# High and low parts of the tokens side by side: one matmul of 512 columns with the weights' high part in place of two of 256

## The chip, the cores and the metric

One core of one Trainium2 chip. The metric is the device time of one execution in microseconds; times are medians of repeated runs.

## What is computed

A decoder trunk of two layers on 256 tokens of width 1024, all in float32. Layer 0 mixes tokens by latent attention, layer 1 by block attention with a learned bias by distance; with 256 tokens there is one block, so it is causal attention over all keys. Behind each mixer stands an MLP with a squared ReLU:

```python
for i in range(DEPTH):
    h = rms_norm(x, attn_norm[i])
    x = x + mixer(h, ...)            # ends in out @ w_o, 1024 x 1024
    h = rms_norm(x, mlp_norm[i])
    a = relu(h @ w_in)               # 1024 x 4096
    x = x + (a * a) @ w_out          # 4096 x 1024
```

## The kernel before, in words

**Three products for one.** Weights and activations are split into a high part in float32r and the rest, also float32r. A product of two split numbers is `mm3` (L87): high by high, low weight by high token, high weight by low token, three matmuls that add into the same 256 columns of PSUM. The weight block of 128x128 is the loaded operand, the 256 tokens stream past it. In the projections (`lat_mm`, `proj0`, `proj1`) it is the other way round: tokens are loaded, 320, 384 or 512 weight columns stream (`lat_end(latq[t], ...)` streams 384).

**Weights.** All weights come in units of 128x1024 through one list, in order of use. For each, SP issues a DMA into `raw` (four buffers), ACT casts it to `wh` (`hi`, L150) and DVE subtracts to get `wl` (`lo`, L159); wh and wl have seven buffers each. `fill(n)` calls `lo` and `hi` n times. The program is recorded by hand in one order; each engine executes its instructions in that order. So where `fill` stands among the other operations decides what DVE and ACT do first.

**The MLP** (`mlp`, L874 on) runs in two halves r of 16 blocks of 128 hidden features. Each half has a w_in stage of eight steps j, counted from 0 (`first`, L882): two blocks of features, 2 x 8 x 3 matmuls into the two halves of one PSUM bank. Then ACT takes the relu out of PSUM (L900), DVE multiplies it with PSUM (the square-up, L902), ACT casts to a's high part (L904), DVE subtracts to get the low part (L905). In layer 0 and 1 alike, steps 1 to 4 of the first half also square x on ACT (L277), and POOL adds the squares up (L279); behind step 6 a matmul with ones sums over partitions and DVE makes the scale (L919, L920). The w_out stage has eight blocks d of 16 x 3 matmuls (`a` by w_out); DVE multiplies the sum with the scale (y, L936), and POOL adds it to x (L938) in the first half. In the second half `finish` adds it to x and makes h for the next stage, or writes the output.

**Layer 0's MLP also makes layer 1's bias.** In step 5 DVE makes small tables (`bias_tables`, L951 on). Then, once per w_out block, DVE compares positions to a step table `st` (L974); one block later eight small bf16 matmuls of 96 columns read that table, and DVE adds their sums to `bias` in six operations (L987). Blocks 0 to 7 of the first w_out stage make a table each; four more follow in the second half.

**The output projections** (`run_heads`): `o` gathers four blocks of 128 features head by head, `col` makes the other four; each ends in `out_residual`, which adds PSUM to x (L592), makes h's high part on ACT (L586) and its low part hTl on DVE (L588). The first w_in step of the MLP goes through k from 0 to 7 for both feature blocks at once and so wants the last h late.

Of the kernel before, what the change touches and what calls it, by code (L numbers as in the profile page):

```python
# [26 lines left out]
H = 8  # L27
# [33 lines left out]
def trunk(ctx: ExitStack, tc: tile.TileContext, A, out):  # L61
# [189 lines left out]
    hTh = const.tile([P, KD, S], F32R)  # L251
    hTl = const.tile([P, KD, S], F32R)
    room(const, "hT")

# [267 lines left out]
    def head_tiles(l):  # L522

        cm = ExitStack()
        pool = cm.enter_context(tc.tile_pool(name=f"heads{l}", bufs=1))
        r = []
        for c in range(2):
            r.append({n: pool.tile([P, *sh], F32, name=f"{n}{c}")
                      for n, sh in (("k", (HG, S)), ("q", (HG, S)), ("v", (NT, HG, P)))})
        room(pool, f"aT{l}")  # L530
        aT = [pool.tile([P, H, S], F32R, name=f"aT{i}") for i in range(2)]
        return cm, r, aT

    class Head:


        def __init__(self, hd, aT, h, bias, extra=None):
            self.aT = (aT[0][:, h], aT[1][:, h])
# [38 lines left out]
        def values(self):  # L577
            o = ps()
            v, pT = self.hd["v"], self.pT
            mm(o[:, :S], v[:, 0, self.i], pT[:, :S], True, False)  # L580
            mm(o[:, P:S], v[:, 1, self.i], pT[:, S:], False, True)
            nc.scalar.copy(self.aT[0], o[:, :S])
            nc.vector.tensor_sub(self.aT[1], o[:, :S], f32(self.aT[0]))
# [7 lines left out]
    def out_residual(a, d, gname):  # L591
        nc.vector.tensor_add(x[:, d], a, x[:, d])  # L592
        make_h_filled(d, gname)

    def run_heads(hs, proj, post, rows, turn, mid, base, gname, n1):
# [7 lines left out]
        def o(h, ds=range(4)):  # L603
            u = unit(base + h // 2)
            for d in ds:
                if h == 0:
                    accs.append(ps()[:, :S])
                c = (h % 2) * 512 + d * P
                mm3(accs[d], part(u, slice(c, c + P)), hs[h].aT, h == 0, h == H - 1)
                if h == H - 1:  # L610
                    out_residual(accs[d], d, gname)
            if h % 2:
                done(base + h // 2)
# [3 lines left out]
        def col(d, hh):  # L617
            if d not in late:
                late[d] = ps()[:, :S]
            u = unit(base + d)  # L620
            for h in hh:
                mm3(late[d], part(u, slice(h * P, (h + 1) * P)), hs[h].aT, h == 0, h == H - 1)
            if hh[-1] == H - 1:
                done(base + d)
                out_residual(late[d], d, gname)
# [248 lines left out]
    def mlp(l, base, fillers, finish):  # L874

        with tc.tile_pool(name=f"mlp{l}", bufs=1) as pool:
            scale = pool.tile([P, S], F32, name="scale")
            room(pool, "a")
            a = [pool.tile([P, 2 * NPAIR, S], F32R, name=f"a{i}") for i in range(2)]
            sums = SumSquares()  # L880

            def first(b, r, j, split_k):  # L882
                u = [unit(b + 2 * j + i) for i in range(2)]
                if split_k:
                    o = [ps()[:, :S] for _ in range(2)]
                else:
                    p = ps()
                    o = [p[:, f * S:(f + 1) * S] for f in range(2)]
                for f, k in [(f, k) for k in range(KD) for f in range(2)] if split_k else \
                        [(f, k) for f in range(2) for k in range(KD)]:  # L890
# [6 lines left out]
                for f, n in ((0, 1), (1, 1)) if split_k else ((0, 2),):  # L897
                    src = o[f] if split_k else p
                    rl = t2(n * S)
                    nc.scalar.activation(rl, src, AF.Relu)  # L900
                    sq = t2(n * S)
                    nc.vector.scalar_tensor_tensor(sq, src, 0.0, rl, op0=OP.max, op1=OP.mult)  # L902
                    ah, al = (i[:, 2 * j + f:2 * j + f + n].rearrange("p a b -> p (a b)") for i in a)
                    nc.scalar.copy(ah, sq)  # L904
                    nc.vector.tensor_sub(al, sq, f32(ah))  # L905
                done(b + 2 * j + 1)

            for r in range(NR):
                b = base + r * (2 * NPAIR + 2 * KD)
                for j in range(NPAIR):  # L910
# [5 lines left out]
                    if r == 0 and j == 6:  # L916
                        pb = ps()
                        mm(pb[:, :S], ones, s, True, True)
                        nc.vector.tensor_scalar(scale, pb[:, :S], 1.0 / D, EPS, op0=OP.mult, op1=OP.add)  # L919
                        nc.vector.reciprocal(scale, scale)  # L920
                b += 2 * NPAIR
                for d in range(KD):
                    o = ps()[:, :S]
                    for f in range(2 * NPAIR):
                        u = unit(b + 2 * d + f // 8)
                        c = (f % 8) * P
                        mm3(o, part(u, slice(c, c + P)), (a[0][:, f], a[1][:, f]), f == 0, f == 2 * NPAIR - 1)
# [8 lines left out]
                    nc.vector.tensor_tensor(y, o, scale, op=OP.mult)  # L936
# [219 lines left out]
```

## Time and profile before

| | us |
|---|---|
| median of 3 runs | 575.67 (575.59 to 576.53) |
| the profiled execution | 575.54 |
| its span, first to last instruction | 573.4 |
| PE busy, 4346 matmuls | 566.9 |
| PEld (weight loads) busy | 540.6 |
| DVE busy | 406.8 |
| ACT busy | 308.4 |
| POOL busy | 109.5 |

The granted clock of TensorE is 0.999 of its full 2.4 GHz over the span. PE's busy time is that of pipelined matmuls, whose ends are modelled: a matmul of 256 columns is shown as 280 ns long, while the next starts much earlier. What a matmul costs is therefore read as the distance from start to start. Two instructions of DVE or ACT behind each other overlap by some 0.08 us, so there too starts tell more than durations.

### The profile page before, as it was taken

The page shows a single profiled execution, that of the slowest core. Times are in us where ns is not written, and L with a number is a line of the kernel's source. Part 1 is how long each engine was busy: PE and PEld are TensorE (multiplying, and loading weights), DVE is VectorE, ACT ScalarE, POOL GpSimd, SP SyncE. Part 2 cuts the span into 40 slices and gives each one's busy share as a digit, 9 for nine tenths or more (in the row PEclk, how much of TensorE's full clock was granted, in tenths as well). Part 3 has the DMA queues.
Part 4 walks back from the last instruction along what each step waited for, and adds up shares of the span by engine and source line. Part 5 has one row for each costly group of instructions (what it writes and reads, how often), then busy time and mean ns, then how long its engine had stood idle before and what let it go on. Part 6 is the DMA issues. An engine that isn't in the chain of part 4 may idle for free.

```text
span 573.4 us, 10762 instructions
## 1 busy us (share of the span) xinstructions
PE 566.9 (99%) x4346; PEld 540.6 (94%) x4346; DVE 406.8 (71%) x654; ACT 308.4 (54%) x495; POOL 109.5 (19%) x107
## 2 busy tenths in 40 slices
PE   8999999999999999999999999999999999999997
PEld 6888999999999999999988888999999999999996
DVE  5997777588999978687647466776777655666651
ACT  5989676664423455454645466745664434555420
POOL 3882100040223100123413101000221322000100
PEclk9999999999999999999999999999999999999999
DMA  8833455554665555665635544345465575465730
GB/s 289 298 118 124 135 155 156 169 173 154 214 177 177 152 187 179 221 229 174 200 132 177 189 149 146 112 147 184 151 201 197 188 196 173 153 212 174 230 123 29
DMA packets 29265, 99.54 MB, mean 174 GB/s; under 512 B 3904, under 2 KB 4800, under 8 KB 29216
## 3 DMA queue, kind: packets, MB, share of 16 engines
q1 hardware_dynamic: 28736, 97.92, 53.4%
q0 software_dynamic: 336, 0.92, 0.5%
q8 instruction: 34, 0.56, 0.4%
q14 instruction: 15, 0.12, 0.1%
q10 hardware_dynamic: 144, 0.02, 0.0%
HBM read 97.79 MB, written 1.05 MB: 172 GB/s over the span
## 4 chain that ended last, share of the span: by engine, by line
PE 96%; DMA 2%; SPq 1%; DVE 0%; issue 0%; ACT 0%
PE ps L85 93%; PE ps L350 1%; DMA xs<-in_x_tok 1%; DMA win<-in_w_in 1%; PE ps L573 1%; SPq L204 0%; SPq L139 0%; PE ps L490 0%; DVE wl L159 0%; ACT wh L150 0%; DVE t L936 0%; DVE t L1002 0%; SPq L206 0%; ACT sqj L455 0%; PE ps L855 0%
## 5 line engine op out<-in xcount | busy, mean ns | idle before, releaser
L150 ACT CAST wh<-raw 128x1024 fp32r<-128x1024 f32 x177 | 183.4, 1047 | 111.6 <-DMA raw<-in_w_out_mlp 61.4
L159 DVE TENSOR_TENSOR wl<-raw,wh 128x1024 fp32r<-128x1024 f32 x177 | 226.9, 1311 | 6.4 <-ACT wh L150 6.0
L85 PE MATMUL ps<-a,wh 128*128 128x256 f32 x1024 | 183.5, 280 | 0.0
L85 PEld LDWEIGHTS ps<-a,wh 128*128 128x128 f32 x1024 | 157.2, 188 | 0.0
L85 PE MATMUL ps<-hTh,wh 128*128 128x256 f32 x512 | 143.8, 281 | 0.0
L85 PE MATMUL ps<-hTh,wl 128*128 128x256 f32 x512 | 143.1, 279 | 0.0
L85 PE MATMUL ps<-a,wl 128*128 128x256 f32 x512 | 142.9, 279 | 0.0
L85 PE MATMUL ps<-hTl,wh 128*128 128x256 f32 x512 | 142.8, 279 | 0.0
L85 PEld LDWEIGHTS ps<-hTh,wh 128*128 128x128 f32 x512 | 96.2, 188 | 0.1
L85 PEld LDWEIGHTS ps<-hTl,wh 128*128 128x128 f32 x512 | 96.0, 188 | 0.0
L85 PEld LDWEIGHTS ps<-hTh,wl 128*128 128x128 f32 x512 | 95.9, 187 | 0.1
L85 PEld LDWEIGHTS ps<-a,wl 128*128 128x128 f32 x512 | 95.8, 187 | 0.0
L85 PE MATMUL ps<-aT,wh 128*128 128x256 f32 x256 | 51.0, 289 | 0.0
L85 PE MATMUL ps<-wh,hTh 128*128 128x512 f32 (+2 forms) x128 | 46.9, 392 | 1.0 <-ACT wh L150 1.0
L85 PE MATMUL ps<-wl,hTh 128*128 128x512 f32 (+2 forms) x128 | 45.1, 378 | 0.1
L85 PE MATMUL ps<-wh,hTl 128*128 128x512 f32 (+2 forms) x128 | 45.1, 379 | 0.0
L938 POOL TENSOR_TENSOR x<-t,x 128x256 f32<-128x256 f32 x16 | 26.4, 1650 | 94.3 <-DVE t L936 94.3
L902 DVE SCALAR_TENSOR_TENSOR t<-ps,t 128x512 f32<-128x512 f32 (+1 forms) x34 | 22.4, 657 | 28.9 <-ACT t L900 28.9
L936 DVE TENSOR_TENSOR t<-ps,scale 128x256 f32<-128x256 f32 x32 | 13.5, 421 | 38.8 <-PE ps L85 38.8
L85 PEld LDWEIGHTS ps<-aT,wh 128*128 128x128 f32 x256 | 40.5, 188 | 0.2
L905 DVE TENSOR_TENSOR a<-t,a 128x512 fp32r<-128x512 f32 (+1 forms) x34 | 22.5, 661 | 22.5 <-ACT a L904 22.5
L904 ACT CAST a<-t 128x512 fp32r<-128x512 f32 (+1 forms) x34 | 20.2, 595 | 32.8 <-DVE t L902 32.8
(167 smaller groups left out, 653.0 us busy)
## 6 DMA issues: line engine op xcount, KB each, us to landing
raw<-in_w_in_mlp SPq DMA_DIRECT2D x64, 512.0 KB, 4.2
raw<-in_w_out_mlp SPq DMA_DIRECT2D x64, 512.0 KB, 4.2
raw<-in_w_qkv SPq DMA_DIRECT2D x24, 512.0 KB, 4.1
raw<-in_w_u SPq DMA_DIRECT2D x8, 512.0 KB, 4.5
win<-in_w_in SPq DMA_DIRECT2D x7, 352.0 KB, 5.9
raw<-in_w_o0a SPq DMA_DIRECT2D x4, 512.0 KB, 3.6
raw<-in_w_o0b SPq DMA_DIRECT2D x4, 512.0 KB, 3.5
raw<-in_w_o1a SPq DMA_DIRECT2D x4, 512.0 KB, 3.8
```

The lines of the kernel that those rows point to most:

```text
L85: nc.tensor.matmul(o, a, b, start=start, stop=stop)
L150: (eng.copy if eng is nc.scalar else eng.tensor_copy)(his[i][:, :w], raws[i][:, :w])
L159: eng.tensor_sub(los[i][:, :w], raws[i][:, :w], f32(his[i][:, :w]))
L350: nc.tensor.transpose(pt[:, i * P:(i + 1) * P], yf[:, i * P:(i + 1) * P], ident)
L573: nc.tensor.transpose(pt[:, i * P:(i + 1) * P], self.p[:, i * P:(i + 1) * P], ident)
L902: nc.vector.scalar_tensor_tensor(sq, src, 0.0, rl, op0=OP.max, op1=OP.mult)
L904: nc.scalar.copy(ah, sq)
L905: nc.vector.tensor_sub(al, sq, f32(ah))
L936: nc.vector.tensor_tensor(y, o, scale, op=OP.mult)
L938: nc.gpsimd.tensor_add(x[:, d], y, x[:, d])
```

## The change

High and low part of tokens now lie beside each other (`hT2`, `aT`, `a` with a dimension of 2), and `mm_both` replaces `mm3`: the weight's high part streams both halves, 512 columns, into a whole PSUM bank; the low part streams the high tokens, 256 columns, into its first half. What was one sum in 256 columns is now two, which are added when they leave PSUM. In `first`, ACT copies the second half to SBUF and DVE adds the first (`half`), once per feature block, and relu and square-up read that sum from SBUF. In w_out, ACT copies, DVE adds, then multiplies. In `out_residual`, DVE adds both halves to x. The calls of `fill` are placed anew: one in the middle of a w_in step, one between cast and subtraction; `out_residual` takes the four blocks of `o` together with one `fill` in place of four. The scale is made in w_out block 0 in place of step 6. The last block of layer 1 keeps `mm3`.

```diff
+    def mm_both(o, w, x2, start, stop):
+        mm(o, w[0], x2, start, False)
+        mm(o[:, 0], w[1], x2[:, 0], False, stop)
+
+    def ps2():
+        return ps().rearrange("p (a b) -> p a b", b=S)
...
-    def out_residual(a, d, gname):
-        nc.vector.tensor_add(x[:, d], a, x[:, d])
-        make_h_filled(d, gname)
+    def out_residual(a, ds, gname):
+        for d in ds:
+            for i in range(2):
+                nc.vector.tensor_add(x[:, d], a[d][:, i], x[:, d])
+            nc.scalar.activation(hTh[:, d], x[:, d], AF.Copy, scale=gain(gname, d))
+        fill()
+        for d in ds:
+            nc.vector.scalar_tensor_tensor(hTl[:, d], x[:, d], gain(gname, d), f32(hTh[:, d]),
+                                           op0=OP.mult, op1=OP.subtract)
...
             def first(b, r, j, split_k):
...
-                    mm3(o[f], part(u[k // 4], slice(c, c + P)), hT(k), k == 0, k == KD - 1)
-                fill(2)
+                o = [ps2() for _ in range(2)]
+                def half(f):
+                    nc.scalar.copy(sm[:, f], o[f][:, 1])
+                    nc.vector.tensor_add(sm[:, f], o[f][:, 0], sm[:, f])
...
+                    mm_both(o[f], part(u[k // 4], slice(c, c + P)), hT2[:, k], k == 0, k == KD - 1)
+                    if i == KD - 1:
+                        if not split_k:
+                            half(0)
+                        fill()
+                for f in range(split_k ^ 1, 2):
+                    half(f)
                 for g in fillers:
                     if g[0] == (r, j):
                         g[1]()
...
+                rl = t2(2, S)
+                nc.scalar.activation(rl, sm, AF.Relu)
+                sq = t2(2, S)
+                nc.vector.scalar_tensor_tensor(sq, sm, 0.0, rl, op0=OP.max, op1=OP.mult)
+                ah, al = (a[:, 2 * j:2 * j + 2, i] for i in range(2))
+                nc.scalar.copy(ah, sq)
+                if j < NPAIR - 1:
+                    fill()
+                nc.vector.tensor_sub(al, sq, f32(ah))
+                if j == NPAIR - 1:
+                    fill()
...
                     if r == 0 and j == 6:
                         pb = ps()
                         mm(pb[:, :S], ones, s, True, True)
-                        nc.vector.tensor_scalar(scale, pb[:, :S], 1.0 / D, EPS, op0=OP.mult, op1=OP.add)
-                        nc.vector.reciprocal(scale, scale)
...
+                        if last:
+                            mm3(o[:, 0], part(u, slice(c, c + P)), (a[:, f, 0], a[:, f, 1]), f == 0, f == 2 * NPAIR - 1)
+                        else:
+                            mm_both(o, part(u, slice(c, c + P)), a[:, f], f == 0, f == 2 * NPAIR - 1)
                         if f == 7:
                             fill()
                             done(b + 2 * d)
+                            if r == 0 and d == 0:
+                                nc.vector.tensor_scalar(scale, pb[:, :S], 1.0 / D, EPS, op0=OP.mult, op1=OP.add)
+                                nc.vector.reciprocal(scale, scale)
...
-                    nc.vector.tensor_tensor(y, o, scale, op=OP.mult)
+                    if last:
+                        nc.vector.tensor_tensor(y, o[:, 0], scale, op=OP.mult)
+                    else:
+                        nc.scalar.copy(y, o[:, 1])
+                        nc.vector.tensor_add(y, o[:, 0], y)
+                        nc.vector.tensor_mul(y, y, scale)
```

The change also moves instructions. DVE in layer 0's first w_out stage, one block, before (`t` is y, `st` the step table, the two `wl` the block's weights):

```order
L936 TENSOR_TENSOR t_2209<-ps,scale 128x256
L159 TENSOR_TENSOR wl<-raw,wh 128x1024 x2
L987 TENSOR_TENSOR bias<-ps,mask 128x8x16
L987 TENSOR_TENSOR bias<-ps,bias 128x8x16 x2
L974 TENSOR_TENSOR st<-steps_q,steps_k 128x1024
```

The same place now:

```order
L968 TENSOR_TENSOR t_2145<-ps,t_2145 128x256
L969 TENSOR_TENSOR t_2145<-t_2145,scale 128x256
L168 TENSOR_TENSOR wl<-raw,wh 128x1024 x2
L1020 TENSOR_TENSOR bias<-ps,mask 128x8x16
L1020 TENSOR_TENSOR bias<-ps,bias 128x8x16 x2
L1007 TENSOR_TENSOR st<-steps_q,steps_k 128x1024
```

The order is the same; the operation that made y has become two, the second of which reads what the first writes. (The mask and bias rows stand twice in a block.)

DVE in a w_in step (j 2 of layer 0, before with the head of j 3); before, L902 is the square-up and L905 the low part of a:

```order
L902 SCALAR_TENSOR_TENSOR t_1535<-ps,t_1533 128x512
L905 TENSOR_TENSOR a_1324<-t_1535,a_1323 128x512
L159 TENSOR_TENSOR wl<-raw,wh 128x1024 x2
L902 SCALAR_TENSOR_TENSOR t_1605<-ps,t_1603 128x512
L905 TENSOR_TENSOR a_1324<-t_1605,a_1323 128x512
```

The same step now; L902 is the add of the two halves, L921 the square-up, L926 the low part of a:

```order
L902 TENSOR_TENSOR t_1392<-ps,t_1392 128x256
L168 TENSOR_TENSOR wl<-raw,wh 128x1024
L902 TENSOR_TENSOR t_1392<-ps,t_1392 128x256
L921 SCALAR_TENSOR_TENSOR t_1437<-t_1392,t_1435 128x512
L168 TENSOR_TENSOR wl<-raw,wh 128x1024
L926 TENSOR_TENSOR a<-t_1437,a 128x2x256
```

Of the two `wl` that stood behind the low part of a, one now stands between the two adds and one between square-up and subtraction.

## Rows read from the trace of the kernel before

**Rows 1.** The page: busy us (share), instructions; chain by engine.

```profile
PE 566.9 (99%) x4346; PEld 540.6 (94%) x4346; DVE 406.8 (71%) x654; ACT 308.4 (54%) x495; POOL 109.5 (19%) x107
...
PE 96%; DMA 2%; SPq 1%; DVE 0%; issue 0%; ACT 0%
```

**Rows 2.** Busy by stage: start:end, length, PE, PEld, DVE, ACT, POOL, clock, DMA.

```profile
139.90:188.00 48.10, 48.10 (x441) 47.79 (x440) 45.55 (x70) 18.17 (x19) 11.55 (x7) 1.00 0.59 178
...
433.40:478.70 45.30, 45.30 (x387) 45.30 (x386) 27.58 (x27) 18.28 (x19) 11.54 (x7) 1.00 0.66 201
```

**Rows 3.** PE's timeline (start, duration): layer 1, first and last end of w_out.

```profile
433.44 0.28 PE L85 MATMUL ps<-a,wh 128*128 128x256 f32 x1
...
478.67 0.28 PE L85 MATMUL ps<-hTh,wh 128*128 128x256 f32 x1
```

**Rows 4.** Chain of waits, in order of time: start, us, what.

```profile
20.96 1.05 PE ps L85 x6
...
310.64 11.20 PE ps L85 x48
...
321.84 0.44 PE ps L350 x4
```

**Rows 5.** DVE's timeline, layer 1, the MLP's scale.

```profile
430.34 0.42 DVE L919 TENSOR_SCALAR scale<-ps 128x256 f32<-128x256 f32 x1
...
430.79 1.75 DVE L920 RECIPROCAL scale<-scale 128x256 f32<-128x256 f32 x1
```

**Rows 6.** DVE's timeline, layer 0, first w_out stage, one block.

```profile
182.00 0.29 DVE L987 TENSOR_TENSOR bias<-ps,mask 128x128 f32<-128x128 f32 x1
...
183.71 1.22 DVE L974 TENSOR_TENSOR st<-steps_q,steps_k 128x1024 bf16<-128x1024 f32 x1
...
184.85 0.42 DVE L936 TENSOR_TENSOR t<-ps,scale 128x256 f32<-128x256 f32 x1
...
185.18 2.89 DVE L159 TENSOR_TENSOR wl<-raw,wh 128x1024 fp32r<-128x1024 f32 x2
...
188.08 0.29 DVE L987 TENSOR_TENSOR bias<-ps,mask 128x128 f32<-128x128 f32 x1
```

**Rows 7.** PE's timeline, same stage, small bias matmuls after blocks 1 and 7.

```profile
151.22 0.51 PE L85 MATMUL ps<-parts,st 128*128 128x96 bf16 x8
...
187.70 0.51 PE L85 MATMUL ps<-parts,st 128*128 128x96 bf16 x8
```

**Rows 8.** Timelines of ACT and DVE, layer 1, first w_in stage.

```profile
393.29 0.39 ACT L900 ACTIVATE t<-ps 128x256 f32<-128x256 f32 x1 [1.39 <-PE ps L85]
...
406.30 0.62 ACT L904 CAST a<-t 128x512 fp32r<-128x512 f32 x1 [0.76 <-DVE t L902]
...
406.83 0.63 ACT L277 ACTIVATE t<-x 128x512 f32<-128x512 f32 x1
...
407.36 1.98 ACT L150 CAST wh<-raw 128x1024 fp32r<-128x1024 f32 x2
...
405.58 0.69 DVE L902 SCALAR_TENSOR_TENSOR t<-ps,t 128x512 f32<-128x512 f32 x1 [1.31 <-ACT t L900]
...
424.93 2.35 DVE L159 TENSOR_TENSOR wl<-raw,wh 128x1024 fp32r<-128x1024 f32 x2
```

**Rows 9.** DVE and POOL, same stage, a sum of squares beside wl.

```profile
413.22 3.46 DVE L159 TENSOR_TENSOR wl<-raw,wh 128x1024 fp32r<-128x1024 f32 x2
...
413.25 2.33 POOL L279 TENSOR_TENSOR ssum<-ssum,t 128x512 f32<-128x512 f32 x1 [4.43 <-ACT t L277]
```

**Rows 10.** DVE, layer 0, w_in step 5, bias tables to square-up.

```profile
129.07 0.83 DVE L951 CAST steps_q<-pos_row 128x256 f32<-128x256 int32 x1
...
131.40 0.68 DVE L902 SCALAR_TENSOR_TENSOR t<-ps,t 128x512 f32<-128x512 f32 x1
```

**Rows 11.** PE and DVE, layer 1: first w_in matmul, last hTl.

```profile
387.79 0.28 PE L85 MATMUL ps<-hTh,wh 128*128 128x256 f32 x1
...
390.50 0.48 DVE L588 SCALAR_TENSOR_TENSOR hTl<-x,gains,hTh 128x256 fp32r<-128x256 f32 x1
```

More of the change, by code (lines that the diff above doesn't have):

```diff
@@ L249, in rsqrt_into @@
                                 if len(t.shape) == 3 else mhalf[:, :n], op=OP.pow)
-    hTh = const.tile([P, KD, S], F32R)
-    hTl = const.tile([P, KD, S], F32R)
+    hT2 = const.tile([P, KD, 2, S], F32R)
     room(const, "hT")
+    hTh, hTl = hT2[:, :, 0], hT2[:, :, 1]
     def make_h(k, gname):
@@ L530, in head_tiles @@
         room(pool, f"aT{l}")
-        aT = [pool.tile([P, H, S], F32R, name=f"aT{i}") for i in range(2)]
+        aT = pool.tile([P, H, 2, S], F32R, name="aT")
         return cm, r, aT
@@ L537, in __init__ @@
         def __init__(self, hd, aT, h, bias, extra=None):
-            self.aT = (aT[0][:, h], aT[1][:, h])
+            self.aT = aT[:, h]
             self.i = h % HG
@@ L581, in values @@
             mm(o[:, P:S], v[:, 1, self.i], pT[:, S:], False, True)
-            nc.scalar.copy(self.aT[0], o[:, :S])
-            nc.vector.tensor_sub(self.aT[1], o[:, :S], f32(self.aT[0]))
+            nc.scalar.copy(self.aT[:, 0], o[:, :S])
+            nc.vector.tensor_sub(self.aT[:, 1], o[:, :S], f32(self.aT[:, 0]))
     def make_h_filled(k, gname):
@@ L618, in col @@
             if d not in late:
-                late[d] = ps()[:, :S]
+                late[d] = ps2()
             u = unit(base + d)
             for h in hh:
-                mm3(late[d], part(u, slice(h * P, (h + 1) * P)), hs[h].aT, h == 0, h == H - 1)
+                mm_both(late[d], part(u, slice(h * P, (h + 1) * P)), hs[h].aT, h == 0, h == H - 1)
             if hh[-1] == H - 1:
                 done(base + d)
-                out_residual(late[d], d, gname)
+                out_residual(late, [d], gname)
         if mid is not None:
@@ L878, in mlp @@
             room(pool, "a")
-            a = [pool.tile([P, 2 * NPAIR, S], F32R, name=f"a{i}") for i in range(2)]
+            a = pool.tile([P, 2 * NPAIR, 2, S], F32R, name="a")
             sums = SumSquares()
@@ L883, in first @@
                 u = [unit(b + 2 * j + i) for i in range(2)]
[L884 to L890, printed above, removed]
-                    c = (k % 4) * 256 + f * P
-                    mm3(o[f], part(u[k // 4], slice(c, c + P)), hT(k), k == 0, k == KD - 1)
-                fill(2)
+                o = [ps2() for _ in range(2)]
+                def half(f):
+                    nc.scalar.copy(sm[:, f], o[f][:, 1])
+                    nc.vector.tensor_add(sm[:, f], o[f][:, 0], sm[:, f])
+                sm = t2(2, S)
+                for i, (f, k) in enumerate([(f, k) for k in range(KD) for f in range(2)] if split_k else
+                                           [(f, k) for f in range(2) for k in range(KD)]):
+                    c = (k % 4) * 256 + f * P
+                    mm_both(o[f], part(u[k // 4], slice(c, c + P)), hT2[:, k], k == 0, k == KD - 1)
[5 more added lines that the diff above has]
+                    half(f)
                 for g in fillers:
@@ L896, in first @@
                         g[1]()
[L897 to L905, printed above, removed]
+                rl = t2(2, S)
[9 more added lines that the diff above has]
+                    fill()
                 done(b + 2 * j + 1)
@@ L918, in mlp @@
                         mm(pb[:, :S], ones, s, True, True)
-                        nc.vector.tensor_scalar(scale, pb[:, :S], 1.0 / D, EPS, op0=OP.mult, op1=OP.add)
-                        nc.vector.reciprocal(scale, scale)
                 b += 2 * NPAIR
                 for d in range(KD):
-                    o = ps()[:, :S]
+                    last = l == 1 and r == NR - 1 and d == KD - 1
+                    o = ps2()
                     for f in range(2 * NPAIR):
```

9 lines of the change are left out of this document (4 added, 5 removed).

## The prediction

> **What bounds the kernel now.** I read the page's busy times and its chain first, then busy time by stage, then the timelines of PE and DVE in the second half of layer 0's MLP, and last the short rows that carry prices. The chain that ends last is TensorE for 96% of the span, and PE is busy 99% of it [rows 1]. So the time is the sum of the intervals at which matmuls follow each other, plus whatever stops PE. Weight loads (PEld) are busy 94%, DVE 71%, ACT 54%. The mean of DVE hides one stretch: in layer 0's first w_out stage it works 45.55 of 48.10 us [rows 2]. That is where an engine that is not the bound now is nearest to being it.
>
> **What a removed matmul is worth.** 384 matmuls of 256 columns take from 433.44 to 478.67 us [rows 3], 117.8 ns each. 48 of 512 columns take 11.20 us, 233.3 ns each; six of 384 columns 1.05 us, 175 ns [rows 4]. The three lie on one line: 117.8 + 115.5 for each further 256 columns, which gives 175.5 at 384. A matmul costs its columns and about 2.3 ns more. Three passes of 256 cost 353.4 ns now; one of 512 and one of 256 would cost 233.3 + 117.8 = 351.1. The columns stay, one load and 2.3 ns go. The pairs: 128 in each of the eight MLP half-stages (1024), less the last output block that keeps three passes (16), and 64 in each of the two output projections: 1136. **Gain: 1136 x 2.3 = 2.6 us.**
>
> **What is added to DVE and ACT.** Each MLP stage of eight w_in steps j gets, per step, two ACT copies of 256 columns out of PSUM and two DVE adds; each w_out block d gets one ACT copy and turns one DVE operation into two that depend on each other. Two dependent operations of 256 columns start 0.45 us apart, the 430.34 and the 430.79 row [rows 5], so a w_out block costs DVE 0.45 us more. Whether that matters is a question of the place.
>
> *Layer 0, first w_out stage.* DVE runs one block after another without idle: six bias adds from 182.00, the step table st 183.71, y 184.85, two wl from 185.18, the next block's bias adds 188.08 [rows 6]. That is 6.08 us per block. PE also takes 6.08 us per block, (187.70 - 151.22) / 6 [rows 7]: 48 x 0.1178 = 5.65 for the matmuls and 0.43 around the eight small bias matmuls. Those read st of the block before; st ends at 184.93, 2.8 us before PE wants it at 187.70. After the change DVE needs 6.08 + 0.45 = 6.53, PE 16 x 0.3511 + 0.43 = 6.05. DVE falls back 0.48 us per block, and once the 2.8 us are used PE stands in front of the small matmuls, with everything behind them.
>
> The 2.8 us shrink before that. The scale (0.45 and then 1.75, which overlaps its follower: 2.1 us, [rows 5]) moves from w_in step 6 into block 0, ahead of st. And w_in hands over late:
>
> *The w_in steps.* One loop now goes through both engines, add, relu, square-up, cast, wh, copy of the next step, add, wl: 0.42 [rows 6], then 0.63 (like the 512-column pass from SBUF), 0.69, 0.62, 1.0, 0.39, 0.42, 1.17 [rows 8], 5.34 and some 0.1 less for overlaps, 5.2 us against 16 x 0.3511 = 5.62 of PE. That fits. With the sum of squares on ACT behind the cast (0.53 net) it is 5.7, and where POOL adds the squares, DVE's wl is held: two wl take 3.46 us beside a POOL add and 2.35 alone [rows 8, 9]; about half of those 1.1 us falls on this loop, so 6.2. Lag behind PE: 0.1 at step 2, and 0.6 for each of three more, 1.9 at step 5; then 0.4 and, with PE's extra 0.3 us for the sum over partitions, 0.7 are won back: 0.8 us at step 7. In layer 0 the bias tables stand between add and square-up in step 5, 2.33 us [rows 10] in place of a wait of 0.7: 2.4 us at step 7.
>
> *From w_in to w_out.* The last a is ready 0.39 + 0.42 + 0.63 + 0.69 + 0.62 + 0.69 + 0.2 (hand-overs) = 3.65 us plus the lag after PE's last w_in matmul; PE wants it after 14 x 0.351 = 4.9 us. Layer 1: 4.4, no stall. Layer 0: 6.05, **1.15 us**. From there, counted from the end of w_in: two wl 2.3, scale 2.1, wl 1.13, st 1.13, so st of block 0 at 12.7 where PE is there at 12.5: **0.2 us**. The next st comes 6.53 later, 19.25; PE, held to 12.7, is there at 12.7 + 0.34 + 5.71 = 18.75: **0.5 us**. Six more tables at 0.48: **2.9 us**. In the second w_in stage the loop of 5.2 wins back what bias work does not eat (six bias adds are 1.7 us, of which 0.7 replaces the wait for relu); I get 1.9 us of lag at its last step, a ready at 5.55 against 4.9: **0.65 us**. Layer 1 has no bias work: its first w_out stage keeps DVE busy 27.58 of 45.30 us [rows 2], so with 8 x 0.45 + 2.1 more there is 1.5 us to spare per block.
>
> *Output projections.* Each of the eight x updates gets a second dependent add (0.37 to 0.45 us), and three wl fewer are asked for there. hTl of the last block is ready at 390.98 now, 3.2 us after PE's first w_in matmul at 387.79 [rows 11]; with the adds and the four halves done in a batch I get 5.0. Today only the third pass of a step wants hTl, now the first does, 14 x 0.351 = 4.9 us in: **0.1 us** per layer.
>
> The wl and wh casts are issued one unit earlier than before, which covers a DVE that is 6 us late, so I count nothing for them. ACT is busy 54% of the span and 18.17 of 48.10 us in the stage above [rows 1, 2], and its wh casts wait for DMAs that are sooner when wl no longer comes in pairs: nothing. PSUM goes from one bank per w_in step to two of eight, four steps deep: nothing. SP and POOL issue what they did.
>
> **Sum:** -2.6 + 1.15 + 0.2 + 0.5 + 2.9 + 0.65 + 0.2 = +3.0 us. The profiled execution took 575.54 us (span 573.4), 0.13 below the median of 575.67: 578.6 us.
>
> **The rivals.** *No lag at the hand-over (575.3).* If the w_in loop keeps up with PE, st of block 0 ends at 3.65 + 2.3 + 2.1 + 2.3 = 10.3 against 11.3, the 1.0 us covers two blocks, and five at 0.48 remain: 2.4 - 2.6 = -0.2, no change. For it: nothing shows ACT and DVE chained like this today, so the lag is worked out and not seen. Against: three POOL adds and the bias tables are in the rows.
>
> *The table stays early (573.1, other side).* One mechanism: in w_out DVE's second wl is held by POOL's x add, two wl 2.90 us against 2.35 [rows 6, 8]. If the added operation shifts POOL's add out from under wl, the block costs DVE 6.53 - 0.55 = 5.98, under PE's 6.05; the point is 6.05. Then the table never comes late, and of the stalls little more than the first remains while the 2.6 us are won: 573.1 with the lag also small. Against it: y, wl, wl stand in the same order as before, so POOL starts at the same point.
>
> *The lag reaches layer 1 (581.6).* If ACT's wh cast, which is inside the loop, waits for its DMA, each of the steps 2 to 5 grows further; 1.5 us more lag costs about 1.2 us at layer 1's hand-over, 1.5 in layer 0's, and 0.3 at the sum over partitions: +3.
>
> *The loads bind (565).* Were the 256-column interval set by its load, then behind a 512-column pass, under which the load is hidden, it could fall towards the shortest interval that fp32 rows show, 0.44 us for four 128-column transposes, 110 ns [rows 4]: 7.8 + 2.3 = 10.1 ns x 1136 = 11.5 us, 564 and some DVE stalls on top. Against it: the line through 256, 384 and 512 columns, where each matmul has one load whatever its width. The Trainium skill, Perfetto Trace Analysis, Identifying the Most-Contended Engine, says to judge TensorE by the share of time in LDWEIGHTS rather than by matmul busy time; at 94% that speaks for this rival, and the line speaks against.
>
> *The 512-column pass overlaps (441).* If 512 columns cost what 256 do, each pair would take 2 x 117.8 ns and save 117.8: 1136 of them 134 us, 441 us. The rows with 233.3 ns in this very kernel all but exclude it. The Trainium skill, TensorE: Matmul & The Clock Gate, Back-to-back issue gap, gives 131 ns per matmul of 512 columns in a sustained stream; by that figure the estimate would be some 457 us, and the trace disagrees.
>
> **How the numbers follow.** The forecast with stalls in layer 0: 0.45; no lag, 575.3: 0.17; the table stays early, 573.1: 0.22; layer 1 too, 581.6: 0.10; the loads bind: 0.05; overlap: 0.01. 0.2% is 1.15 us, about what a measurement of this kernel can tell from no change. Faster: 0.22 + 0.05 + 0.01 = 0.28; same: 0.17; slower: 0.45 + 0.10 = 0.55. The range goes from half a microsecond under the early table, 572.6, to just over the layer 1 case, 582.0, and leaves out the last two rivals and the tails. The likeliest case's own range is 576.9 to 580.3 (each of the four layer 0 terms half or half as much again).
>
> **What would show it.** Right: pairs at 351 ns in layer 1's MLP, stages there 0.3 us shorter; in layer 0's first w_out stage, PE idle ahead of the bias matmuls with DVE's st as releaser, 0.4 to 0.5 us per block from block 1 or 2, DVE with no idle at 6.5 us per block; a gap after 14 pairs of block 0. Wrong: a 256-column interval under 115 ns; st still ahead of PE at block 7; gaps in layer 1; wl as releaser.

## The result and the profile after

| | before | after |
|---|---|---|
| median, us (6 runs each) | 575.63 (575.51 to 576.53) | 580.97 (579.46 to 581.35) |
| ratio, 95% interval | | 1.0087 [1.0077, 1.0097] |
| the profiled execution | 575.54 | 581.25 |
| its span | 573.4 | 579.5 |

The change makes the kernel 5.3 us slower, where +3.0 was forecast. The times of one kernel with the pairs can stand in two groups some 1.5 us apart (the change: 579.5 and 580.9 to 581.4; layer 0's MLP as before, below: 574.0 to 574.3 and 575.3 to 576.3), and the profiled execution of the change is of the longer group, 6.0 us over that of before in its span.

The page of after, first busy times, then the chain by engine; the same lines of before are [rows 1]:

```profile
PE 567.8 (98%) x3210; PEld 487.5 (84%) x3210; DVE 443.5 (77%) x761; ACT 332.2 (57%) x586; POOL 103.3 (18%) x107
...
PE 72%; DVE 19%; ACT 3%; issue 3%; DMA 1%; POOL 1%; SPq 1%; ACTq 0%; DVEq 0%; POOLq 0%
```

1136 matmuls and as many loads are gone: 4346 less 1136 is 3210, and PEld falls by 53 us. PE's busy time is what it was. The chain, all but pure PE before, now goes through DVE for 19% of the span. Where, the length of each stage tells, from the first matmul of a stage to the first of the next:

| stage | before | after | difference |
|---|---|---|---|
| up to layer 0's MLP | 94.25 | 94.91 | +0.66 |
| layer 0, w_in, first half | 45.66 | 45.63 | 0.0 |
| layer 0, w_out, first half | 48.12 | 51.93 | +3.81 |
| layer 0, w_in, second half | 46.59 | 46.95 | +0.36 |
| layer 0, w_out, second half | 46.08 | 47.38 | +1.30 |
| layer 1's projections and heads | 107.08 | 107.03 | -0.05 |
| layer 1, w_in, first half | 45.66 | 45.59 | -0.07 |
| layer 1, the three other stages | 135.56 | 135.59 | +0.03 |

5.5 of the 6.0 us are layer 0's MLP. Where nothing stands in the way, in layer 1, 0.1 us is won. After's busy times by stage, with the columns of [rows 2]: layer 0's four stages, then layer 1's first w_out:

```profile
94.90:140.50 45.60, 45.37 (x260) 39.48 (x259) 36.60 (x59) 29.33 (x49) 5.51 (x4) 1.00 0.55 169
140.50:192.50 52.00, 49.36 (x315) 41.45 (x313) 49.29 (x81) 23.71 (x32) 9.94 (x6) 1.00 0.55 176
...
192.50:239.40 46.90, 46.69 (x284) 40.35 (x282) 43.72 (x74) 26.25 (x45) 2.39 (x2) 1.00 0.55 172
239.40:286.80 47.40, 46.23 (x274) 40.00 (x273) 34.11 (x53) 23.13 (x36) 11.81 (x8) 1.00 0.58 186
439.40:484.70 45.30, 45.30 (x259) 39.47 (x258) 34.19 (x38) 21.79 (x29) 11.57 (x7) 1.00 0.66 207
```

DVE works 49.29 of 52.00 us in the second line, and PE is idle there for 2.6 us. In the last line PE is never idle, at a granted clock of 1.00 as before, with 128 matmuls and loads fewer, and still needs the 45.30 us of [rows 2]. What PE waits for in the whole span (us in total, times, longest):

```profile
PE ps L85 <- DVE st L1007: 2.8, 8, 1.2
PE ps L85 <- ACT wh L159: 1.8, 2, 1.2
PE ps L85 <- DVE a L926: 1.2, 1, 1.2
PE ps L85 <- DVE zeros L202: 1.2, 1, 1.2
PE ps L85 <- DVE hT L607: 0.2, 1, 0.2
```

Before it had only wh and zeros, at the start. Such a wait is counted from the modelled end of the matmul before, some 0.16 us after the next could have started (0.28 less the 0.118 of [rows 3]), so each costs more than the list says: the first w_out stage of layer 0 is 3.81 us longer with 2.6 us of waits. PE's timeline in layer 0's first w_out stage, the wait for `a` and the first three rows of small matmuls (L85 with `parts`), which answer to [rows 7]; the rows behind them look like the last:

```profile
146.87 0.51 PE L85 MATMUL ps<-a,wh 128*128 128x512 f32 x1 [1.22 <-DVE a L926]
...
153.47 0.51 PE L85 MATMUL ps<-parts,st 128*128 128x96 bf16 x8
159.91 0.52 PE L85 MATMUL ps<-parts,st 128*128 128x96 bf16 x8 [0.27 <-DVE st L1007]
166.35 0.52 PE L85 MATMUL ps<-parts,st 128*128 128x96 bf16 x8 [0.21 <-DVE st L1007]
```

And DVE in one block there, which answers to [rows 6]:

```profile
177.98 1.22 DVE L1007 TENSOR_TENSOR st<-steps_q,steps_k 128x1024 bf16<-128x1024 f32 x1
179.11 0.42 DVE L968 TENSOR_TENSOR t<-ps,t 128x256 f32<-128x256 f32 x1
179.56 0.42 DVE L969 TENSOR_TENSOR t<-t,scale 128x256 f32<-128x256 f32 x1
179.90 2.90 DVE L168 TENSOR_TENSOR wl<-raw,wh 128x1024 fp32r<-128x1024 f32 x2
182.73 0.28 DVE L1020 TENSOR_TENSOR bias<-ps,mask 128x128 f32<-128x128 f32 x1
...
184.42 1.22 DVE L1007 TENSOR_TENSOR st<-steps_q,steps_k 128x1024 bf16<-128x1024 f32 x1
```

From st to st it is 6.44 us where it was 6.08, without an idle moment, and PE's small matmuls follow at the same 6.44. DVE sets the pace of this stage from its second table on.

In layer 0's second w_out stage it is one wait. DVE, the tables of blocks 0 and 2 and what stands ahead of the latter; then PE:

```profile
247.49 1.22 DVE L1007 TENSOR_TENSOR st<-steps_q,steps_k 128x1024 bf16<-128x1024 f32 x1
...
261.35 1.22 DVE L168 TENSOR_TENSOR wl<-raw,wh 128x1024 fp32r<-128x1024 f32 x1 [0.97 <-ACT wh L159]
262.50 1.22 DVE L1007 TENSOR_TENSOR st<-steps_q,steps_k 128x1024 bf16<-128x1024 f32 x1
```

```profile
263.77 0.51 PE L85 MATMUL ps<-parts,st 128*128 128x96 bf16 x8 [1.17 <-DVE st L1007]
```

Before, that table ended 2.95 us ahead of its matmuls; now they wait for it.

What a pair costs can be read in layer 1's first w_out stage, whose 128 pairs answer to [rows 3]:

```profile
439.42 0.40 PE L85 MATMUL ps<-a,wh 128*128 128x512 f32 x1
...
444.30 0.49 PE L85 MATMUL ps<-a,wh 128*128 128x512 f32 x1
...
444.75 0.39 PE L85 MATMUL ps<-a,wh 128*128 128x512 f32 x1
...
484.67 0.40 PE L85 MATMUL ps<-hT,wh 128*128 128x512 f32 x1
```

The first 14 pairs take 4.88 us, 349 ns each. The next, the first that reads the last `a`, takes 0.45, with a pause of some 0.09 us. The 113 behind it take 39.92 us, 353.3 ns each, what three passes of 256 cost. The stream has two paces, and over most of this execution it runs at the slower one, at the same granted clock (1.00, that is 2.4 GHz).

### The profile page after: what moved, and what is told of

Its sections match the earlier page's. It is cut to its first block, busy times and chain, and to the rows that moved or that the text cites. A ratio compares the mean times of both kernels' runs of the same rounds, so it can differ in the third digit from the quotient of the medians.

```text
span 579.5 us, 8701 instructions
## 1 busy us (share of the span) xinstructions
PE 567.8 (98%) x3210; PEld 487.5 (84%) x3210; DVE 443.5 (77%) x761; ACT 332.2 (57%) x586; POOL 103.3 (18%) x107
## 4 chain that ended last, share of the span: by engine, by line
PE 72%; DVE 19%; ACT 3%; issue 3%; DMA 1%; POOL 1%; SPq 1%; ACTq 0%; DVEq 0%; POOLq 0%
PE ps L85 69%; DVE wl L168 8%; DVE bias L1020 3%; DVE st L1007 2%; ACT wh L159 2%; PE ps L359 1%; DVE t L902 1%; DMA rowp<-in_rowp 1%; DVE t L921 1%; PE ps L582 1%; DVE x L603 1%; DVE t L968 1%; DVE hT L607 1%; POOL x L1027 1%; ACT t L919 0%
## 5 line engine op out<-in xcount | busy, mean ns | idle before, releaser
L85 PE MATMUL ps<-a,wh 128*128 128x512 f32 (+1 forms) x528 | 182.2, 390 | 1.2 <-DVE a L926 1.2
L85 PE MATMUL ps<-hT,wh 128*128 128x512 f32 x512 | 181.6, 397 | 0.2 <-DVE hT L607 0.2
L85 PE MATMUL ps<-a,wl 128*128 128x256 f32 x512 | 144.3, 282 | 0.0
L85 PE MATMUL ps<-hT,wl 128*128 128x256 f32 x512 | 144.3, 282 | 0.0
L85 PEld LDWEIGHTS ps<-a,wh 128*128 128x128 f32 x528 | 98.2, 188 | 23.6 <-DVE a L926 1.5
L85 PEld LDWEIGHTS ps<-hT,wh 128*128 128x128 f32 x512 | 96.2, 188 | 23.2 <-DVE hT L607 0.6
L85 PEld LDWEIGHTS ps<-hT,wl 128*128 128x128 f32 x512 | 96.3, 188 | 0.1
L85 PEld LDWEIGHTS ps<-a,wl 128*128 128x128 f32 x512 | 96.3, 188 | 0.0
L85 PE MATMUL ps<-wh,hT 128*128 128x512 f32 (+2 forms) x256 | 74.6, 386 | 1.8 <-ACT wh L159 1.8
L85 PEld LDWEIGHTS ps<-wh,hT 128*128 128x128 f32 x256 | 46.3, 190 | 11.3 <-ACT wh L159 2.6
L85 PE MATMUL ps<-aT,wh 128*128 128x512 f32 x128 | 48.3, 414 | 0.0
L85 PE MATMUL ps<-wl,hT 128*128 128x512 f32 (+2 forms) x128 | 45.2, 378 | 0.1
L902 DVE TENSOR_TENSOR t<-ps,t 128x256 f32<-128x256 f32 x64 | 26.8, 421 | 17.9 <-ACT t L901 17.9
L921 DVE SCALAR_TENSOR_TENSOR t<-t,t 128x512 f32<-128x512 f32 x32 | 22.1, 691 | 19.1 <-ACT t L919 19.1
L85 PE MATMUL ps<-aT,wl 128*128 128x256 f32 x128 | 36.0, 281 | 0.0
```

Of the source, the lines that this page charges most:

```text
L85: nc.tensor.matmul(o, a, b, start=start, stop=stop)
L902: nc.vector.tensor_add(sm[:, f], o[f][:, 0], sm[:, f])
L921: nc.vector.scalar_tensor_tensor(sq, sm, 0.0, rl, op0=OP.max, op1=OP.mult)
```

## The experiments

All but the third operation, which was executed once, were timed beside the kernel before, whose median lay between 575.38 and 575.51. Below, "the change" is the kernel after. Stage lengths come from the profiled execution of each kernel and stand in the order layer 0 w_in, w_out, w_in, w_out, and the same for layer 1.

### The merge undone

```diff
-        mm(o, w[0], x2, start, False)
+        mm(o[:, 0], w[0], x2[:, 0], start, False)
+        mm(o[:, 1], w[0], x2[:, 1], False, False)
```

> The changed kernel with the 512-column pass split into two of 256 columns with the same high weight, so three loads and three passes per weight block as in the kernel before; the separate halves, the added ACT and DVE work and the new places of fill stay. Prediction's line (2.3 ns per matmul): PE gives 2.6 us back, 583 to 584 us, pairs of 351 become triples of 353.4 ns. Rival (time goes by columns, a merged pass is worth next to nothing; the profile of the changed kernel shows 353.3 ns per pair over most of the span and 348.9 in one stretch): within 1.2 us of the changed kernel, 580 to 582 us, triples of 353.3 ns everywhere, and layer 0's w_out stalls as they are.

580.39 us (580.00 to 580.46), ratio 1.0086 [1.0071, 1.0101]; layer 1's stages 45.66, 45.23, 45.22, 45.11. That is within the range of the change, 0.6 us under its median, with 1136 more matmuls and loads: the rival was right. In the median the merge is worth nothing; the 2.6 us of the forecast are missing. Every triple takes 353.4 ns here, as before, where a pair takes 353.3 or 349: the merge gains 4.5 ns or nothing, by the pace that a stretch has. One small gain stands in every profile: from the first matmul of layer 0's output projection to its MLP it is 33.1 to 33.2 us with pairs and 33.4 with triples.

### The old end of a w_out block, in layer 0's first w_out stage alone

```diff
-                    last = l == 1 and r == NR - 1 and d == KD - 1
+                    last = (l == 1 and r == NR - 1 and d == KD - 1) or (l == 0 and r == 0)
```

> The changed kernel, with the eight blocks of layer 0's first w_out stage back to three passes of 256 into one sum, and one DVE operation for y in place of copy, add and multiply. Theory (the second dependent operation of a block makes the step table late): DVE's block falls from 6.44 to 6.08 us, PE waits for the table at block 0 or 1 at most, the stage goes from 51.9 us to 48.5 to 49.5, and the kernel to 577 to 578.5 us. Rival (the lag handed over by w_in and the moved scale make the whole stall): the stage stays above 50.5 us, the kernel above 579.5.

577.13 us (575.04 to 577.70), ratio 1.0021 [1.0010, 1.0032]. The stage takes 49.42 us in place of 51.93, and PE waits 0.9 us for st in the whole span in place of 2.8. The two stages behind it are shorter as well, 46.26 and 46.49 in place of 46.95 and 47.38. One DVE operation per block in one stage, with the ACT copy and the pairs that go with it, makes 3.8 of the 5.3 us. This is what the theory expected.

### The step table ahead of the bias adds

```diff
-    fillers.sort(key=lambda f: f[1].__name__ == "steps")
+    fillers.sort(key=lambda f: f[1].__name__ != "steps")
```

> The changed kernel with the order inside a w_out block (and a w_in step of the second half) turned: DVE makes the step table before the six bias adds of the block before, not after them. No work is added or taken away. Theory (PE waits for the table, DVE's block of 6.44 us is longer than PE's 6.08): the table is ready 1.7 us earlier at every block, so PE starts to wait some four blocks later; of 3.8 us in that stage 1.5 to 2.5 go, kernel 578.5 to 579.8 us, and the waits that stay fall in the last blocks. Rival (DVE's total work sets the pace whatever the order, through wl or through the hand-over): no change, 580.5 to 581.5.

580.67 us (579.36 to 580.91), ratio 1.0087 [1.0072, 1.0102], the time of the change: the rival was right. PE's waits for the table in this stage fall to 0.2 us and the stage by 2.06 us to 49.87, but the next two grow by 0.46 and 1.19 to 47.41 and 48.57, where PE now waits for `a` (0.9 us) and wl (0.4) too. The wait is not won by an earlier table: DVE is behind with its work, and PE waits for it later.

### The 256-column pass first

```diff
+        if start:
+            mm(o, w[0], x2, True, False)
+            mm(o[:, 0], w[1], x2[:, 0], False, stop)
+        else:
+            mm(o[:, 0], w[1], x2[:, 0], False, False)
+            mm(o, w[0], x2, False, stop)
```

> The changed kernel with the order inside a pair turned for all but the first pair of a sum: the low weight's 256 columns first, then the high weight's 512. Columns, loads and all other engines the same. Theory that time goes by columns and by a state of PE's that only the stream decides: pairs of 353.3 ns or of 348.9 ns as in the changed kernel, in other stretches, 578 to 582 us. Rival (the step from a 512-column pass to a 256-column one, and its load, is what costs): the interval after a 256-column pass changes by over 3 ns, PE's stages in layer 1 by over 0.3 us each.

579.79 us (579.59 to 579.98), ratio 1.0077 [1.0062, 1.0092]; layer 1's stages 45.24, 45.34, 44.78, 44.87. The change has 45.59, 45.25, 45.22 and 45.11: three of the stages are shorter by 0.24 to 0.45 us, with the same columns and loads. So these alone do not set the pace. That this order does is not shown, for the order of the change has stages as short where it runs at its faster pace (44.73, 44.66 and 44.61 in the profile of the version above, with the table first).

### Layer 0's MLP as before, the pairs elsewhere

```diff
+            def first_old(b, r, j, split_k):
...
-                    first(b, r, j, r == 0 and j == 0)
+                    (first if l else first_old)(b, r, j, r == 0 and j == 0)
...
-                    last = l == 1 and r == NR - 1 and d == KD - 1
+                    last = l == 0 or r == NR - 1 and d == KD - 1
```

(`first_old` is the old `first`, with `mm3` and one fill per step; the scale goes back to step 6 in layer 0.)

> The changed kernel with layer 0's MLP as it was before (three passes into one sum, old evacuations, old places of fill and scale); layer 1's MLP and both output projections keep the pairs. Theory (all of the loss is DVE's added work in layer 0; a pair costs 353.3 or 348.9 ns by PE's pace, against 353.4 for three passes): layer 0's four MLP stages within 0.3 us of the kernel before, layer 1's between 44.7 and 45.3 us each, PE waiting 0.3 us at most in layer 1, kernel 573 to 575.8 us. Rival (the pairs or the projections lose time by themselves): 576.5 us or more.

575.43 us (574.02 to 576.29), ratio 0.9996 [0.9987, 1.0005]. The loss is gone in the median, so it lies in layer 0's MLP, and the 624 pairs that remain, each with a load and a matmul saved, bring nothing there.

### A third operation per block

```diff
+                        if l == 0 and r == 0:
+                            nc.vector.tensor_scalar(y, y, 1.0, None, op0=OP.mult)
```

> The changed kernel with a third dependent DVE operation per block (a multiplication of y by 1.0) in layer 0's first w_out stage, eight in all. Theory (DVE's block sets PE's pace there): DVE's block grows from 6.44 to 6.8 or 6.9 us and PE's with it, the stage from 51.9 to 54.7 to 55.7 us, 3 to 3.6 us, and the lag handed to the second half adds up to 1 us more. Rival (DVE has slack there and something else stops PE): under 1 us more in all.

583.43 us in a single execution; the stage takes 53.53 us, 1.6 more. PE's small matmuls there now follow at 6.76 us:

```profile
159.97 0.51 PE L85 MATMUL ps<-parts,st 128*128 128x96 bf16 x8 [0.60 <-DVE st L1009]
166.73 0.52 PE L85 MATMUL ps<-parts,st 128*128 128x96 bf16 x8 [0.52 <-DVE st L1009]
```

More DVE work lengthens the stage, block for block; the size was overestimated. This operation, out of SBUF, takes 0.29 us, not 0.42, and the block grew by 0.32, not 0.4. And PE meets its first wait for a table at the same place in both, 19.4 us into the stage; five blocks behind it at 0.32 are the 1.6 us.

### The scale back at w_in step 6

```diff
                     if r == 0 and j == 6:
                         pb = ps()
                         mm(pb[:, :S], ones, s, True, True)
+                        nc.vector.tensor_scalar(scale, pb[:, :S], 1.0 / D, EPS, op0=OP.mult, op1=OP.add)
+                        nc.vector.reciprocal(scale, scale)
...
-                            if r == 0 and d == 0:
-                                nc.vector.tensor_scalar(scale, pb[:, :S], 1.0 / D, EPS, op0=OP.mult, op1=OP.add)
-                                nc.vector.reciprocal(scale, scale)
```

> The changed kernel with the scale made behind w_in step 6 again, as before, and not in w_out block 0. Prediction's sums: 2.1 us of DVE work move from behind the hand-over to ahead of it. The lag at step 7 grows by 2.1, so PE waits some 2 us longer for a, and the table of block 0 comes no earlier: the stage ends within 0.7 us of the changed kernel's, in layer 0; in layer 1 a new wait for a of 1 to 1.8 us appears in each kernel run: 581 to 583 us. Rival (w_in has slack enough for it): the table comes 2 us earlier, 579 us.

582.30 us (582.20 to 582.45), ratio 1.0120 [1.0105, 1.0134]. PE now waits in front of both first w_out stages, 2.8 us in layer 0 and 1.6 in layer 1 (whose stage takes 47.05 us in place of 45.25):

```profile
PE ps L85 <- DVE a L926: 4.4, 2, 2.8
PE ps L85 <- DVE st L1006: 1.6, 3, 1.2
```

The place of the scale that the change chose is worth 1.3 us, and the loop of ACT and DVE behind w_in has no 2.1 us to spare in either layer.

### Two by two

Layer 0 as before; in layer 1's MLP the 512-column passes of two weight blocks, then their two 256-column passes.

```diff
+    def mm_two(o, w, x2, start, stop):
+        held.append((o, w, x2, start, stop))
+        if len(held) == 2:
+            for h in held:
+                mm(h[0], h[1][0], h[2], h[3], False)
+            for h in held:
+                mm(h[0][:, 0], h[1][1], h[2][:, 0], False, h[4])
+            held.clear()
```

> As the kernel with layer 0's MLP as before, but in layer 1's MLP two 512-column passes follow each other, then the two 256-column passes of the same two weight blocks. Columns and loads the same. If an interval depends on its own width alone (233.3 after 512 where 512 follows, 117.8 after 256 where 256 follows): 351.1 ns per pair, stages of 44.95 us, 0.3 us less each than with pairs at the slow pace. If the pace of 353.3 or 348.9 ns per pair is a state of the stream whatever its order: stages of 45.2 or 44.7 us.

572.80 us (572.11 to 572.97), ratio 0.9951 [0.9939, 0.9963]: faster than both kernels. Layer 1's stages take 44.79, 45.03, 44.16 and 44.17 us, the second with a wait of 0.60 for `a`; the last two are shorter than any that was expected. Its second and third by engine (columns as in [rows 2]), and PE's timeline in the second:

```profile
433.30:478.30 45.00, 44.40 (x258) 38.93 (x257) 34.81 (x40) 22.61 (x30) 11.59 (x7) 1.00 0.64 209
478.30:522.50 44.20, 44.20 (x259) 38.93 (x258) 32.93 (x46) 28.27 (x45) 0.74 (x1) 1.00 0.57 174
```

```profile
452.11 0.62 PE L85 MATMUL ps<-a,wh 128*128 128x512 f32 x2
452.57 0.39 PE L85 MATMUL ps<-a,wl 128*128 128x256 f32 x2
452.80 0.62 PE L85 MATMUL ps<-a,wh 128*128 128x512 f32 x2
...
453.49 0.62 PE L85 MATMUL ps<-a,wh 128*128 128x512 f32 x2
```

Two pairs in 0.69 us, 345 ns each, 8 less than one by one at the slower pace and 4 less than at the faster. The same matmuls and loads at the same granted clock, in another order.

### Eight by eight

```diff
-        if len(held) == 2:
+        if len(held) == 8:
```

> As the kernel with two 512-column and two 256-column passes in turn in layer 1's MLP (345 ns per pair, 572.8 us), but eight and eight. If what counts is how often the stream changes between a 512- and a 256-column pass (once per pair: 353.3 or 348.9 ns, half as often: 345), a quarter as often again should come to some 342 ns, stages of 43.8 us, kernel 571.5 us. Rival (the pace of two by two is one of a few that a stream falls into): no steady fall, 345 or above, 572.5 to 574 us.

573.12 us (572.87 to 573.73), ratio 0.9958 [0.9943, 0.9973]. No more than two by two, and PE waits 1.4 us for `a` at the hand-over, since all of a block's 512-column passes now come early. In PE's timeline a row groups eight matmuls:

```profile
452.92 1.07 PE L85 MATMUL ps<-a,wl 128*128 128x256 f32 x8
453.83 1.99 PE L85 MATMUL ps<-a,wh 128*128 128x512 f32 x8
455.66 1.11 PE L85 MATMUL ps<-a,wl 128*128 128x256 f32 x8
456.60 0.62 PE L85 MATMUL ps<-a,wh 128*128 128x512 f32 x2
```

From start to start eight passes of 256 take 0.91 us the first time, 114 ns each, and 0.94 the next, 118 ns; eight of 512 take 1.83, 229 ns each, twice 114. The 118 of a 256-column pass, on which the forecast built its line, is one of two values.

### The kernel before, two weight blocks at a time

```diff
+    def mm3_two(o, a, b, start, stop):
+        held.append((o, a, b, start, stop))
+        if len(held) == 2:
+            for h in held:
+                mm(h[0], h[1][0], h[2][0], h[3], False)
+            for h in held:
+                mm(h[0], h[1][1], h[2][0], False, False)
+            for h in held:
+                mm(h[0], h[1][0], h[2][1], False, h[4])
+            held.clear()
```

> The kernel before, with the three passes of two neighbouring weight blocks taken together: high by high twice, low weight twice, low token twice, all 256 columns wide; the first w_in step of each MLP and the projections stay. If the order of operands (which kind of tile is loaded and streamed next to which) sets the pace, the triple falls from 353.4 to about 345 ns, 8 us in all, 567 to 569 us. Rival (the gain needs passes of 512 columns; all intervals of a stream with one width are alike): 353.3 ns per triple, 575.2 to 575.8 us.

575.48 us (575.29 to 575.91), ratio 1.0000 [0.9990, 1.0009], each stage as before within 0.1 us. This order changes nothing while every pass has 256 columns.

### The change, two by two in both layers

```diff
-                    mm_both(o[f], part(u[k // 4], slice(c, c + P)), hT2[:, k], k == 0, k == KD - 1)
+                    (mm_both if split_k else mm_two)(o[f], part(u[k // 4], slice(c, c + P)), hT2[:, k], k == 0, k == KD - 1)
...
-                            mm_both(o, part(u, slice(c, c + P)), a[:, f], f == 0, f == 2 * NPAIR - 1)
+                            mm_two(o, part(u, slice(c, c + P)), a[:, f], f == 0, f == 2 * NPAIR - 1)
```

> The changed kernel with only the order of passes turned in both MLPs: two 512-column passes, then two 256-column passes. Theory (layer 0's first w_out stage and what follows it go by DVE, layer 1 goes by PE): layer 1's MLP gains 3 to 3.5 us as it did beside the old layer 0, layer 0's first w_in stage about 1, and layer 0's first w_out stage gains nothing, since PE waits for the tables instead: 575.5 to 577.5 us. Rival (PE sets the pace in layer 0 too): 8 us gained, 572 to 573 us.

577.64 us (577.14 to 577.87), ratio 1.0034 [1.0022, 1.0047], just over the range that was expected. Layer 1's stages are those of the version with layer 0 as before (44.78, 45.04, 44.16, 44.18). Layer 0's first w_in stage gains 0.45 us and its first w_out stage loses 0.41 (52.34), because PE, now faster, waits longer for DVE:

```profile
PE ps L85 <- DVE st L1018: 3.9, 8, 1.6
PE ps L85 <- DVE a L937: 3.0, 3, 1.7
```

### The last table one block earlier

```diff
-        r, j = (0, NPAIR + i) if i < KD else (1, (1, 4, 8, 10)[i - KD])
+        r, j = (0, NPAIR + i) if i < KD else (1, (1, 4, 8, 9)[i - KD])
```

> The change with the last bias table made one block earlier in layer 0's second w_out stage (in block 1 in place of block 2; the second-half stages are otherwise as changed). In the change PE stands 1.17 us there, ahead of the small bias matmuls of block 3, because st of block 2 stands on DVE behind a wl whose wh cast waits on ACT behind the steps of finish (POOL's x add, hT, the square). If that queue is the cause: st is ready some 4 us before PE wants it, no wait for st in that stage, stage about 46.2 us instead of 47.38, time 1.0 to 1.3 us under the change, about 579.7. Rival, DVE's lag in layer 0 is paid in any case at the next hand-over: the 1.1 us of the table only delay the wl, hT or the next stage, PE waits about as long for one of those, time as the change, 581.0.

580.97 us (579.39 to 581.49), ratio 1.0090 [1.0077, 1.0104]: no gain. The edit was badly chosen, and the 4 us of its expectation were wrong, for the matmuls that read the table moved one block ahead with it:

```profile
258.35 0.51 PE L85 MATMUL ps<-parts,st 128*128 128x96 bf16 x8 [1.15 <-DVE st L1007]
```

PE meets the same wait a block earlier. So the wait is not tied to that one place, which speaks for DVE's lag at the hand-over rather than for the queue behind `finish`; the two were not parted.

## Why the prediction was right and where it was wrong

**DVE late with the tables: right in mechanism and place, somewhat too large.** 6.53 us per block were forecast, 6.44 measured. The wait of 1.15 us for `a` came as 1.22 (0.85 to 0.97 in the profiles of the third operation, the table first and the earlier table, which have the same w_in steps). Hand-over and tables together were to cost 4.75 us. In the stage's 3.81 the hand-over has 1.6 (the first small matmuls come 12.93 us into the stage in place of 11.31) and six tables have 2.2: 0.36 each, DVE's 6.44 less the 6.08 of PE's own work, where 0.48 was forecast. The last table is read in the next stage, the second w_in, and is its 0.36; 4.2 in all. The old block end alone (-2.5 us in the stage), a third operation (+1.6) and the table ahead of the bias adds, whose wait came back later, show the cause. The rival that had the table stay early falls: POOL's x add still starts under wl (180.06, with wl from 179.90), and two wl still take 2.90 us:

```profile
180.06 1.66 POOL L971 TENSOR_TENSOR x<-t,x 128x256 f32<-128x256 f32 x1 [4.79 <-DVE t L969]
```

The Trainium skill, SBUF — State Buffer, Who interferes with whom, says that a DVE operation with two SBUF inputs contends with a GpSimd operation that reads SBUF; the 2.90 us, against 2.35 for two wl that stand alone, agrees with that.

**The second half: the lag right, the one who waits wrong.** `a` was to be 0.65 us late. It was not: PE takes 353 and not 351 ns per pair, and `a` is there at 244.17, where PE wants it at 244.4. But the table of block 0 ends 9.3 us into the stage where it ended 6.5 in, 2.8 later; three blocks with 0.45 more each would make it 4.2, and the 2.95 us that were to spare with the 1.17 of the wait are 4.1. The stage is 1.30 us longer for the 0.65 of the forecast. I costed the hand-over and did not follow the queue behind it to the next table.

**Layer 1 and ACT: right.** No wait in layer 1's MLP but the pause of 0.09 us at the hand-over. One hT wait of 0.2 us, in layer 0, for 0.1 in each.

**The gain: the step that failed.** "A matmul costs its columns and about 2.3 ns more" took three intervals, each of passes of one width, for the parts of a mixed stream. The pair that was to cost 351.1 ns costs 353 over most of the span and 349 in stretches, and with the merge undone the time is the same. So the 2.6 us did not come, and the forecast of 578.6 is 2.4 us short: 580.97 lies outside the likeliest case's own range (576.9 to 580.3) and near the rival with a lag in layer 1 (581.6), whose wait did not come. That the error is so nearly this one term is luck, for the others have both signs and leave 0.4 us in the profile: 0.6 less than forecast for hand-over and tables, 0.65 more in the second half, 0.66 ahead of layer 0's MLP that no term had, 0.3 less for the projections and layer 1. The Trainium skill, TensorE: Matmul & The Clock Gate, Wait — 56ns, not 53.3ns?, has a fixed 2.5 ns per matmul, nearly my figure; by it the merge would have saved 2.8 us, as an estimate, and the runs disagree in both directions: nothing or 4.5 ns per pair one by one, 8 two by two. The sign that I had named for loads that bind, a 256-column interval under 115 ns, does appear: ten times among some 1040 in the MLPs of the change, each just behind an interruption of the stream, and in 235 of 542 two by two in layer 1. Whether the loads make it was not tried.

**Not foreseen:** 0.66 us ahead of layer 0's MLP. The traces show where: PE starts its first transposes of `ckv` at 20.58 us before and at 21.46 after; from there to the output projection both take 40.3 us, and that projection is 0.25 shorter. In the first 21 us ACT's casts wait for the DMAs of x and w_in, and PE for the casts, 1.8 us where it was 1.0. The other kernels with any of the change reach these transposes between 20.64 and 21.75 us, though they do the same up to there. So most of this differs from one execution to the next; whether the change has a part in it is not shown.

**What stays open:** why the pace is 353, 349 or 345 ns per pair. The runs exclude the count of loads and of matmuls (merge undone) and the granted clock, which is 1.00 throughout; they show that order matters once passes of 512 and 256 columns mix. The traces show also where a pace is settled. In the seven profiles with pairs in the order of the change, none of the stretches of 14 pairs or more that nothing interrupts changes its pace; it changes only where small matmuls, the sum over partitions or a wait come between. In layer 1 the last such place is the hand-over to its first w_out stage, at 444.30 us above. Behind it 352 pairs ran at 353.3 ns in six profiles and at 348.9 in the one with the table first, whose last three stages took 44.73, 44.66 and 44.61 us. 352 x 4.4 ns are 1.5 us, as much as lies between the two groups of times; that fits, but no execution of the change's shorter group was profiled. What in the interruption decides is open.

## What to carry to other kernels

Fewer matmuls for the same columns were no gain by themselves here: the stream has to be timed in the mix and the order in which it will run, and order was worth more here (two by two, 2.7 us in layer 1's MLP) than 1136 matmuls and their loads. A change that adds work to DVE must be priced in the stage where DVE has the least room, and an operation that was moved ahead there only sent the wait on. Where an edit is good in one place and bad in another, it pays to make it only in the first: layer 1 two by two with layer 0 as before is the fastest version, 572.80 us.

## What the runs showed of the hardware that was not expected

A stream of 256-column passes keeps 117.8 ns each in both orders that were tried (before, and two weight blocks at a time). Mixed with passes of 512 columns the same pass can take 114 ns, and the 512 columns 229 instead of 233: 345 ns per pair two by two, 349 or 353 one by one. One by one, an uninterrupted stretch keeps the pace with which it began. PEld's busy share fell from 94 to 84% with the change while the time rose, and in layer 1's first w_out stage PEld worked 39.47 us in place of 45.30 in the same 45.30 us, so that share told nothing of what could be won there.
